# Two attentions of a two-block network: where the softmax scaling runs, how its row statistics are grouped, and how the gates' bias is made

## The chip, the core and the metric

One Trainium2 chip, one core. The metric is the device time of one execution in microseconds, as the median of several runs. The engines of the core are TensorE (PE, with PEld for its weight loads), VectorE (DVE), ScalarE (ACT), GpSimd (POOL) and SyncE (SP), each with its own queue of instructions that it runs in order.

## What is computed

A residual network of depth 2 twice over, on 256 tokens of width 1024, in float32: first a short convolution and an RWKV mixer, each followed by an MLP, then two attentions, each followed by an MLP. The change touches the two attentions alone. Both have 16 heads of 64 and work in two blocks of 128 queries. Cut to what matters:

```python
def dsa_attention(xn, w_in, w_o):            # q, k with rotary position; 4 key heads
    score = einsum(relu(qi . ki), wi)        # an indexer of 8 heads
    _, sel = top_k(where(admissible, score, -inf), 64)
    logits = qg . k[sel] * scale             # masked where a key was not selected
    p = softmax(logits)
    return (p @ v[sel]) @ w_o

def shared_kv(h, g_kv, w_kv, b_f):           # log of the forget gates, summed over the tokens
    cum = cumsum(log_sigmoid(f_logit + b_f))

def fox_attention(xn, w_q, w_o, k, v, cum):
    logits = q . k * scale
    decay = cum[query] - cum[key]
    logits = where(key_pos <= query_pos, logits + decay, -inf)
    p = softmax(logits)
    return (p @ v) @ w_o
```

A term that is the same for all keys of a query, such as `cum[query]`, cancels in the softmax.

## The kernel before

Activations lie transposed, features on the partitions and the 256 tokens along the row. A linear layer reads weights in units of 128x1024. SP loads them in pairs, ACT rounds a unit to the short format (L357, `HL`), DVE takes the remainder (L359), and PE makes each product in three short matmuls (L393 to L395). Units are split three ahead of their use, four split units have room (`HLB`), and three PSUM banks (`mm`) take the results of linear layers.

The code emits the linear layers and the work that hangs on their results interleaved: `drive` emits `per` steps of the linear layer (4 in the first attention, 5 in the second; a step is three matmuls), then one step of each active generator, up to its next `yield`. A planner then orders each engine's queue by this order of emission and by its own estimates of durations, with the weight splits given a head start; the chip runs the queues as they are.

In both attentions the query projection is a linear layer of 8 units, and each unit gives a pair of heads. For a pair, `attend` emits: the scores on PE into PSUM (L828 for the first 128 queries against 128 keys, L829 for the second 128 against all 256); on DVE, for each head and block, the bias added and the row's maximum (L836, which writes `lg`), then the maximum scaled (L839, `nm`); on ACT the exponentials with their sums (L844); on DVE the reciprocal (L847, `rs`) and the scaling of `lg` by it (L849), one instruction for 128x128 and one for 128x256 a head; on PE the transposes (L855); on ACT their copy (L857); on PE the product with the values (L862, L863); on ACT and DVE the split of the result (L865, L866). `lg` has four buffers, enough for two pairs.

In the first attention (`dsa`, called DSA below) the indexer's top-k runs on DVE before the first maximum can be taken; the mask `madd` (L1010) is the bias of all heads. The queries are rotated: DVE makes one product (L934), POOL the other (L933) and their sum `q` (L935), for which the scores wait. In the second (`fox`) the bias is made for each head on DVE (L1126) from the gates of the keys `cb` (broadcast to all partitions by a DMA through DRAM, L1096), those of the queries `cq` (two transposes on PE, L1100, and L1101) and the causal mask `cm`. POOL has no work there.

Of the kernel before, what the change touches and what calls it, by code (L numbers as in the profile page):

```python
# [6 lines left out]
F32 = mybir.dt.float32  # L7
F32R = mybir.dt.float32r
AF = mybir.ActivationFunctionType
OP = mybir.AluOpType  # L10
# [159 lines left out]
def att_consts():  # L170

    d = np.arange(128) % 64
    inv = (1.0 / (10000.0 ** (np.arange(0, 64, 2, dtype=np.float32) / np.float32(64)))).astype(np.float32)
    ang = (np.arange(T, dtype=np.float32)[None] * inv[d // 2][:, None]).astype(np.float32)
    cos, sin = np.cos(ang), np.sin(ang) * np.where(d % 2, 1, -1)[:, None]
    q = np.arange(128)[:, None]
    causal = [np.where(np.arange(w)[None] <= q + o, 0.0, -1e30) for w, o in ((128, 0), (256, 128))]
    return np.concatenate([cos, sin] + causal, axis=1).astype(np.float32)


def stage_units(stage, I):
# [30 lines left out]
def layout(I, stages):  # L212
# [11 lines left out]
    for i in ADAPE:  # L224
# [12 lines left out]
        "cc": col(I["c"].reshape(-1)),  # L237
    }
    a["attc"] = att_consts()
    a["wf"] = I["w_kv_b_2"][:, 2 * D:].reshape(KT, 128, 16).transpose(1, 0, 2).reshape(128, KT * 16)  # L240
    a["wa2"] = np.concatenate([I["rw_w2"][0], I["rw_a2"][0]], axis=0)
# [11 lines left out]
class Prog:  # L253
# [559 lines left out]
        s.at = cx.enter_context(s.tc.tile_pool(name="at", bufs=2))  # L813
        s.at1 = cx.enter_context(s.tc.tile_pool(name="at1", bufs=1))

    def attend(s, i, q, k, v, bias):


        nc = s.nc
        mm, tr = nc.tensor.matmul, nc.tensor.transpose  # L820
        V, A, G = nc.vector, nc.scalar, nc.gpsimd
        E2 = range(2)
        r = [slice(64 * e, 64 * e + 64) for e in E2]
        parts = ((0, 128), (128, 384))
        lg, m, nm, sm, rs, w, ps = ({} for _ in range(7))
        for e in E2:
            ps[e] = s.axbank()
            mm(ps[e][:, 0:128], q[r[e], 0:128], k(e)[:, 0:128], start=True, stop=True)  # L828
            mm(ps[e][:, 128:384], q[r[e], 128:256], k(e), start=True, stop=True)  # L829
        yield  # L830
        for e in E2:
            bb = bias(e)
            lg[e] = s.at.tile([128, 384], F32, name="lg", bufs=4)
            m[e] = s.at.tile([128, 2], F32, name="m", bufs=4)
            for j, (a, b) in enumerate(parts):
                V.tensor_tensor_reduce(lg[e][:, a:b], ps[e][:, a:b], bb[j], scale=1.0, scalar=-3e38, op0=OP.add, op1=OP.max,  # L836
                                       accum_out=m[e][:, j:j + 1])
            nm[e] = s.at.tile([128, 2], F32, name="nm", bufs=4)
            V.tensor_scalar(nm[e], m[e], -0.125, None, op0=OP.mult)  # L839
        yield  # L840
        for e in E2:
            sm[e] = s.at.tile([128, 2], F32, name="sm", bufs=4)
            for j, (a, b) in enumerate(parts):
                A.activation(lg[e][:, a:b], lg[e][:, a:b], AF.Exp, bias=nm[e][:, j:j + 1], scale=0.125,  # L844
                             accum_out=sm[e][:, j:j + 1])
            rs[e] = s.at.tile([128, 2], F32, name="rs", bufs=4)
            V.reciprocal(rs[e], sm[e])  # L847
            for j, (a, b) in enumerate(parts):
                V.tensor_scalar(lg[e][:, a:b], lg[e][:, a:b], rs[e][:, j:j + 1], None, op0=OP.mult)  # L849
            yield  # L850

        for e in E2:
            pt = s.axbank()
            for j in range(3):
                tr(pt[:, 128 * j:128 * j + 128], lg[e][:, 128 * j:128 * j + 128], s.ident)  # L855
            w[e] = s.at.tile([128, 384], F32, name="pt", bufs=4)
            A.activation(w[e], pt[:, :384], AF.Copy)  # L857
        yield
        po = s.axbank()
        for e in E2:  # L860
            kw = dict(tile_position=(0, 64 * e))
            mm(po[r[e], :T], v(e, 0), w[e][:, 0:256], start=True, stop=False, **kw)  # L862
            mm(po[r[e], 128:T], v(e, 1), w[e][:, 256:384], start=False, stop=True, **kw)  # L863
        yield
        A.activation(s.yh[:, i], po[:, :T], AF.Copy)  # L865
        V.tensor_tensor(s.yl[:, i], po[:, :T], s.yh[:, i].bitcast(F32), op=OP.subtract)  # L866
# [21 lines left out]
    def dsa(s, after):  # L888
        nc, tc = s.nc, s.tc
        mm, tr = nc.tensor.matmul, nc.tensor.transpose  # L890
        V, A, G = nc.vector, nc.scalar, nc.gpsimd
        with ExitStack() as cx:
            s.attn_pool(cx)
            at, one = s.at, s.at1
# [3 lines left out]
            ps = s.axbank()  # L898
# [25 lines left out]
            def swapped(raw, n=2):  # L924

                t = s.t("rs")
                for e in range(2):
                    (nc.sync, A, G)[RPQ[e]].dma_start(t[e:64 * n:2], raw[1 - e:64 * n:2])
                return t

            def rope(dst, raw, sw, e):
                u = s.t("ru")
                (V, G)[RPE[e]].tensor_tensor(u, sw, sn, op=OP.mult)  # L933
                V.tensor_tensor(dst, raw, ct, op=OP.mult)  # L934
                (V, G)[RPE[e + 2]].tensor_tensor(dst, dst, u, op=OP.add)  # L935
# [46 lines left out]
            madd = sc[:, 1]  # L982
# [47 lines left out]
            def ev_q(m, ps):  # L1030
                raw = s.t("raw")
                A.activation(raw, ps[:, :T], AF.Copy)
                sw = swapped(raw)
                yield RPW[2]
                q = at.tile([128, T], F32, name="q", bufs=3)
                rope(q, raw, sw, 1)
                yield
                n = m // 2
                s.finish_gen(idx)
                yield from s.attend(m, q, lambda e: kd[64 * e:64 * e + 64, n],  # L1040
                         lambda e, j: vr[:, n // 2, j, 64 * (n % 2):64 * (n % 2) + 64],
                         lambda e: (madd[:, 0:128], madd[:, 128:384]))
            lin(8, ev_q, head=HQ)
        after()
        s.out_proj()
# [15 lines left out]
    def fox(s, after):  # L1061
        nc, tc = s.nc, s.tc
        mm, tr = nc.tensor.matmul, nc.tensor.transpose
        V, A, G = nc.vector, nc.scalar, nc.gpsimd
        with ExitStack() as cx:
            s.attn_pool(cx)
            at, one = s.at, s.at1
            cm = one.tile([128, 384], F32, name="cm")
            G.dma_start(cm, s.d["attc"][:, 2 * T:])
            wf = one.tile([128, KT, 16], F32, name="wf")  # L1070
            G.dma_start(wf.rearrange("p a b -> p (a b)"), s.d["wf"])
# [6 lines left out]
            ps = s.axbank()  # L1078
            for kt in range(KT):
                s.mm3(ps[:16, :T], (wfs[:, 0], wfs[:, 1]), kt, zh[:, kt, :T], zl[:, kt, :T], kt == 0, kt == KT - 1)  # L1080
            f = one.tile([16, 4, T], F32, name="f")
# [12 lines left out]
            nc.sync.dma_start(cd, f[:, 3])  # L1094
            cb = s.big.tile([128, 16, T], F32, name="cb", tag="h1")
            nc.sync.dma_start(cb, bass.AP(tensor=cd.tensor, offset=cd.offset, ap=[[0, 128], [T, 16], [1, T]]))  # L1096
            cq = one.tile([128, 2, 16], F32, name="cq")
            pt = s.axbank()
            for j in range(2):
                tr(pt[:, 16 * j:16 * j + 16], f[:, 3, 128 * j:128 * j + 128], s.ident[:16, :16])  # L1100
            V.tensor_scalar(cq, pt[:, :32].rearrange("p (a b) -> p a b", a=2), -1.0, None, op0=OP.mult)  # L1101
            lin = lambda n, ev, **kw: s.linear(n, lambda k: zh[:, k, :T], lambda k: zl[:, k, :T], ev, per=PERF, **kw)
            kT = one.tile([128, 8, T], F32, name="kT")
            vr = one.tile([128, 8, 2, 128], F32, name="vr")
# [13 lines left out]
            def ev_q(m, ps):  # L1118
                q = at.tile([128, T], F32, name="q", bufs=3)
                V.tensor_tensor(q, ps[:, :T], s.rstd[:, :T], op=OP.mult)  # L1120

                def bias(e):
                    h = 2 * m + e
                    b = at.tile([128, 384], F32, name="fb", bufs=3)
                    for j, (a, w) in enumerate(((0, 128), (128, 256))):
                        V.scalar_tensor_tensor(b[:, a:a + w], cb[:, h, :w], cq[:, j, h:h + 1], cm[:, a:a + w], op0=OP.add,  # L1126
                                               op1=OP.add)
                    return b[:, 0:128], b[:, 128:384]
                yield
                yield from s.attend(m, q, lambda e: kT[64 * e:64 * e + 64, m], lambda e, j: vr[:, m, j, 64 * e:64 * e + 64], bias)  # L1130
            s.linear(8, lambda k: zq[:, 0, k], lambda k: zq[:, 1, k], ev_q, head=HFQ, per=PERF)
# [649 lines left out]
```

## Time and profile before

| what | value |
|---|---|
| median of 3 runs | 1428.42 us (1427.44 to 1430.31) |
| the profiled execution | 1418.36 us |
| its span in the trace | 1416.6 us |
| PE, DVE, ACT, POOL busy | 95%, 70%, 52%, 9% of the span |

The profiled execution is one more execution, 10.06 us below the median of the runs; 1.8 us of its time lie outside the span. The trace tells of that execution alone. DSA's attention proper lies at 846 to 900 us of the span, fox's stage at 1105 to 1207 us, and its attention proper from 1156 us on.

### The profile page before, as it was taken

The numbers are of one execution on the slowest core, as the hardware profiler recorded it, in microseconds if no ns is written. First come the engines' busy times: TensorE is split into PE (matmuls) and PEld (weight loads), VectorE is DVE, ScalarE is ACT, GpSimd is POOL, SyncE is SP. The second block draws the span as 40 slices with busy tenths as digits, with TensorE's granted clock in tenths as the row PEclk, the third lists the DMA queues.
The fourth block names the chain that finished last, engine by engine and source line by source line (L and its number), as shares of the span: only waits on it lengthen the run. The fifth ranks groups of instructions, "written<-read, shape, count | busy, mean of one in ns | idle before, by whom it ended". The sixth has DMA issues, their size and how long they took to land.

```text
span 1416.6 us, 26025 instructions
## 1 busy us (share of the span) xinstructions
PE 1349.4 (95%) x10420; PEld 1290.1 (91%) x10420; DVE 994.1 (70%) x1937; ACT 742.4 (52%) x1424; POOL 132.9 (9%) x157
## 2 busy tenths in 40 slices
PE   6999999997969999999999998999999999999997
PEld 6999999996859998899999986899999987999997
DVE  3699998757875876687566679755557668655554
ACT  3445664842524442267377545674565456673663
POOL 0000000003460212100000254000000000000000
PEclk9999999998989999999999999999999999999999
DMA  8688898556733210266555444355555651455552
GB/s 322 234 329 292 311 324 292 189 199 251 284 133 120 83 53 16 68 220 202 197 185 179 158 143 142 102 183 199 181 179 188 227 181 61 149 208 180 183 198 95
DMA packets 46904, 263.38 MB, mean 186 GB/s; under 512 B 5472, under 2 KB 9776, under 8 KB 20800
## 3 DMA queue, kind: packets, MB, share of 16 engines
q1 hardware_dynamic: 46432, 260.97, 51.9%
q8 instruction: 82, 1.34, 0.4%
q0 software_dynamic: 208, 0.59, 0.1%
q14 instruction: 38, 0.31, 0.1%
q10 hardware_dynamic: 144, 0.16, 0.1%
HBM read 257.69 MB, written 2.11 MB: 183 GB/s over the span
## 4 chain that ended last, share of the span: by engine, by line
PE 76%; DVE 13%; POOL 3%; DMA 3%; issue 2%; ACT 2%; POOLq 0%; DVEq 0%; SPq 0%; ACTq 0%
PE mm L394 19%; PE mm L393 19%; PE mm L395 19%; DVE HL L359 3%; PE mm L391 2%; DVE adu L553 2%; PE mm L430 2%; PE ax L430 1%; DMA raw<-in_w_dram 1%; DMA adu<-in_ada_dram 1%; PE ax L569 1%; PE ax L862 1%; POOL R L1321 1%; PE ax L1372 1%; DMA rs<-raw 1%
## 5 line engine op out<-in xcount | busy, mean ns | idle before, releaser
L359 DVE TENSOR_TENSOR HL<-raw,HL 128x1024 fp32r<-128x1024 f32 x348 | 426.8, 1233 | 226.0 <-ACT HL L357 225.7
L357 ACT ACTIVATE HL<-raw 128x1024 fp32r<-128x1024 f32 x348 | 364.3, 1056 | 281.5 <-PE mm L395 214.9
L395 PE MATMUL mm<-zh,HL 128*128 128x256 f32 (+1 forms) x1328 | 376.5, 284 | 5.5 <-DVE HL L359 5.4
L393 PE MATMUL mm<-zh,HL 128*128 128x256 f32 (+1 forms) x1328 | 377.0, 284 | 2.7 <-ACT cv L663 1.2
L394 PE MATMUL mm<-zl,HL 128*128 128x256 f32 (+1 forms) x1328 | 375.6, 283 | 0.0
L394 PE MATMUL mm<-hlo,HL 128*128 128x256 f32 x1024 | 288.1, 281 | 0.0
L395 PE MATMUL mm<-hh,HL 128*128 128x256 f32 x1024 | 287.8, 281 | 0.0
L393 PE MATMUL mm<-hh,HL 128*128 128x256 f32 x1024 | 285.5, 279 | 0.0
L395 PEld LDWEIGHTS mm<-zh,HL 128*128 128x128 f32 x1328 | 251.9, 190 | 6.9 <-DVE HL L359 6.8
L393 PEld LDWEIGHTS mm<-zh,HL 128*128 128x128 f32 x1328 | 251.8, 190 | 6.1 <-issue 2.4
L394 PEld LDWEIGHTS mm<-zl,HL 128*128 128x128 f32 x1328 | 252.6, 190 | 0.0
L393 PEld LDWEIGHTS mm<-hh,HL 128*128 128x128 f32 x1024 | 193.5, 189 | 0.0
L394 PEld LDWEIGHTS mm<-hlo,HL 128*128 128x128 f32 x1024 | 192.7, 188 | 0.1
L395 PEld LDWEIGHTS mm<-hh,HL 128*128 128x128 f32 x1024 | 192.5, 188 | 0.0
L553 DVE CUSTOM_DVE_ANT_0 adu<-adu,cact,cols 128x1024 f32<-128x1024 f32 x67 | 84.9, 1280 | 0.6 <-DMA adu<-in_ada_dram 0.6
L393 PE MATMUL mm<-yh,HL 128*128 128x256 f32 x256 | 75.5, 297 | 3.1 <-DVE x L718 2.2
L394 PE MATMUL mm<-yl,HL 128*128 128x256 f32 x256 | 74.2, 292 | 0.0
L395 PE MATMUL mm<-yh,HL 128*128 128x256 f32 x256 | 73.8, 289 | 0.0
L523 POOL TENSOR_TENSOR r<-r,mhalf 128x2 f32<-128x2 f32 x6 | 6.3, 1047 | 675.0 <-DVE r L518 542.2
L761 DVE TENSOR_TENSOR hlo<-ma,hh 128x256 fp32r<-128x256 f32 x128 | 53.5, 422 | 5.8 <-ACT hh L758 3.1
L758 ACT ACTIVATE hh<-ma 128x256 fp32r<-128x256 f32 x128 | 52.9, 417 | 3.5
L393 PEld LDWEIGHTS mm<-yh,HL 128*128 128x128 f32 x256 | 50.1, 196 | 4.6 <-issue 3.2
(437 smaller groups left out, 2104.0 us busy)
## 6 DMA issues: line engine op xcount, KB each, us to landing
raw<-in_w_dram SPq DMA_DIRECT2D x177, 1024.0 KB, 4.9
adu<-in_ada_dram SPq DMA_DIRECT2D x72, 512.0 KB, 7.7
rawh<-in_w_dram SPq DMA_DIRECT2D x13, 1024.0 KB, 6.2
raw<-in_ada_dram SPq DMA_DIRECT2D x12, 1024.0 KB, 6.1
cb<-cd SPq DMA_DIRECT2D x1, 2048.0 KB, 10.9
rs<-raw SPq DMA_DIRECT2D x28, 64.0 KB, 1.9
x<-in_x_dram SPq DMA_DIRECT2D x4, 256.0 KB, 4.6
R<-in_wa_dram SPq DMA_DIRECT2D x2, 512.0 KB, 6.8
```

Of the source, the lines that this page charges most:

```text
L357: s.nc.scalar.activation(h, raw, AF.Copy)
L359: s.nc.vector.tensor_tensor(l, raw, h.bitcast(F32), op=OP.subtract)
L391: mm(ps, H[:, kt], rh, start=start, stop=stop)
L393: mm(ps, H[:, kt], rh, start=start, stop=False)
L394: mm(ps, H[:, kt], rl, start=False, stop=False)
L395: mm(ps, L[:, kt], rh, start=False, stop=stop)
L430: s.nc.tensor.matmul(ps[j][:, :N], a, b[:, k], start=kt == i == 0, stop=kt == 7 and i == len(ab) - 1)
L553: s.nc.vector.tensor_tensor_reduce(t, t, s.cact, scale=1.0, scalar=s.c("adab", i), op0=OP.mult, op1=OP.add, accum_out=s.modf[:, i:i + 1])
L569: s.nc.tensor.matmul(ps, w[:, k], s.ccol[:, k:k + 1], start=k == 0, stop=k == KT - 1)
L758: nc.scalar.activation(s.hh[:, m], a, AF.Copy)
L761: nc.vector.tensor_tensor(s.hlo[:, m], a, s.hh[:, m].bitcast(F32), op=OP.subtract)
L862: mm(po[r[e], :T], v(e, 0), w[e][:, 0:256], start=True, stop=False, **kw)
```

## The change

It does four things. The scaling of the exponentials moves from DVE to POOL, for both heads of a pair in fox and for the first head in DSA, where the second stays on DVE (`on_v`). The four maxima, sums and reciprocals of a pair share one tile each, so one instruction scales four maxima and one takes four reciprocals; with that the exponentials of the first head wait for the maxima of both, and the scaling of the first head for the sums of both. In fox the bias of a head is no longer made for each head: two additions over all 16 heads add the causal mask to the first 128 keys' gates (into a new tile `c0`) and to the last 128 (in `cb` itself), and the queries' gates with their two transposes are left out. The causal mask in DRAM is 128 columns wide in place of 384.

```diff
-    causal = [np.where(np.arange(w)[None] <= q + o, 0.0, -1e30) for w, o in ((128, 0), (256, 128))]
-    return np.concatenate([cos, sin] + causal, axis=1).astype(np.float32)
+    causal = np.where(np.arange(128)[None] <= q, 0.0, -1e30)
+    return np.concatenate([cos, sin, causal], axis=1).astype(np.float32)
...
-    def attend(s, i, q, k, v, bias):
+    def attend(s, i, q, k, v, bias, on_v=()):
...
+        m, nm, sm, rs = (s.at.tile([128, 4], F32, name=n, bufs=3) for n in ("m", "nm", "sm", "rs"))
...
             lg[e] = s.at.tile([128, 384], F32, name="lg", bufs=4)
-            m[e] = s.at.tile([128, 2], F32, name="m", bufs=4)
             for j, (a, b) in enumerate(parts):
                 V.tensor_tensor_reduce(lg[e][:, a:b], ps[e][:, a:b], bb[j], scale=1.0, scalar=-3e38, op0=OP.add, op1=OP.max,
-                                       accum_out=m[e][:, j:j + 1])
-            nm[e] = s.at.tile([128, 2], F32, name="nm", bufs=4)
-            V.tensor_scalar(nm[e], m[e], -0.125, None, op0=OP.mult)
+                                       accum_out=m[:, 2 * e + j:2 * e + j + 1])
+        V.tensor_scalar(nm, m, -0.125, None, op0=OP.mult)
         yield
         for e in E2:
-            sm[e] = s.at.tile([128, 2], F32, name="sm", bufs=4)
             for j, (a, b) in enumerate(parts):
-                A.activation(lg[e][:, a:b], lg[e][:, a:b], AF.Exp, bias=nm[e][:, j:j + 1], scale=0.125,
-                             accum_out=sm[e][:, j:j + 1])
-            rs[e] = s.at.tile([128, 2], F32, name="rs", bufs=4)
-            V.reciprocal(rs[e], sm[e])
+                n = slice(2 * e + j, 2 * e + j + 1)
+                A.activation(lg[e][:, a:b], lg[e][:, a:b], AF.Exp, bias=nm[:, n], scale=0.125, accum_out=sm[:, n])
+        V.reciprocal(rs, sm)
+        for e in E2:
             for j, (a, b) in enumerate(parts):
-                V.tensor_scalar(lg[e][:, a:b], lg[e][:, a:b], rs[e][:, j:j + 1], None, op0=OP.mult)
+                (V if e in on_v else G).tensor_scalar(lg[e][:, a:b], lg[e][:, a:b], rs[:, 2 * e + j:2 * e + j + 1], None, op0=OP.mult)
             yield
...
-                         lambda e: (madd[:, 0:128], madd[:, 128:384]))
+                         lambda e: (madd[:, 0:128], madd[:, 128:384]), on_v=(1,))
...
-            cm = one.tile([128, 384], F32, name="cm")
+            cm = one.tile([128, 128], F32, name="cm")
...
-            cq = one.tile([128, 2, 16], F32, name="cq")
-            pt = s.axbank()
-            for j in range(2):
-                tr(pt[:, 16 * j:16 * j + 16], f[:, 3, 128 * j:128 * j + 128], s.ident[:16, :16])
-            V.tensor_scalar(cq, pt[:, :32].rearrange("p (a b) -> p a b", a=2), -1.0, None, op0=OP.mult)
+            c0 = one.tile([128, 16, 128], F32, name="c0")
+            tri = cm[:, None, :].to_broadcast([128, 16, 128])
+            V.tensor_tensor(c0, cb[:, :, :128], tri, op=OP.add)
+            V.tensor_tensor(cb[:, :, 128:], cb[:, :, 128:], tri, op=OP.add)
...
                 def bias(e):
                     h = 2 * m + e
-                    b = at.tile([128, 384], F32, name="fb", bufs=3)
-                    for j, (a, w) in enumerate(((0, 128), (128, 256))):
-                        V.scalar_tensor_tensor(b[:, a:a + w], cb[:, h, :w], cq[:, j, h:h + 1], cm[:, a:a + w], op0=OP.add,
-                                               op1=OP.add)
-                    return b[:, 0:128], b[:, 128:384]
+                    return c0[:, h], cb[:, h]
```

## Rows read from the trace of the kernel before

**Rows 1.** The page's first part: busy time, share of the span and instructions by engine.
```profile
PE 1349.4 (95%) x10420; PEld 1290.1 (91%) x10420; DVE 994.1 (70%) x1937; ACT 742.4 (52%) x1424; POOL 132.9 (9%) x157
```
**Rows 2.** Windows: span; PE, PEld, DVE, ACT, POOL busy (instructions); clock, DMA share, GB/s.
```profile
858.40:867.00 8.60, 5.22 (x45) 4.44 (x46) 7.80 (x31) 5.74 (x21) 4.26 (x4) 1.00 0.45 154
867.00:871.00 4.00, 4.00 (x24) 3.27 (x24) 3.28 (x17) 1.82 (x5) 0.92 (x2) 0.58 0.69 262
871.00:880.00 9.00, 8.17 (x70) 6.34 (x67) 8.26 (x31) 6.44 (x19) 5.87 (x7) 1.00 0.08 27
880.00:900.00 20.00, 19.89 (x139) 14.43 (x138) 14.67 (x74) 14.62 (x53) 1.89 (x3) 1.00 0.16 55
...
1125.00:1156.00 31.00, 31.00 (x172) 26.79 (x171) 16.36 (x21) 13.05 (x15) 0.00 (x0) 1.00 0.64 233
...
1168.00:1176.00 8.00, 7.51 (x61) 6.45 (x61) 7.95 (x33) 4.28 (x10) 0.00 (x0) 1.00 0.16 57
1176.00:1190.00 14.00, 14.00 (x118) 11.22 (x116) 13.62 (x61) 12.05 (x40) 0.00 (x0) 1.00 0.11 44
1190.00:1207.00 17.00, 16.93 (x114) 12.34 (x113) 11.17 (x51) 8.91 (x30) 0.00 (x0) 1.00 0.19 63
```
**Rows 3.** Waits of PE, 846 to 900 us: total, times, longest.
```profile
PE ax L828 <- POOL q L935: 3.4, 2, 2.0
```
**Rows 4.** Timeline of DSA: start, duration, instruction, idle before and its releaser.
```profile
864.50 0.42 DVE L934 TENSOR_TENSOR q<-raw,tabs 128x256 f32<-128x256 f32 x1
...
864.91 1.22 DVE L359 TENSOR_TENSOR HL<-raw,HL 128x1024 fp32r<-128x1024 f32 x1
865.06 1.64 POOL L935 TENSOR_TENSOR q<-q,ru 128x256 f32<-128x256 f32 x1 [4.34 <-DVE nm L839]
...
866.76 0.50 PE L828 MATMUL ax<-kd,q 64*128 64x128 f32 x4 [2.03 <-POOL q L935]
```
**Rows 5.** Groups of DVE by form, 855 to 897 us: busy us, mean ns.
```profile
L849 DVE TENSOR_SCALAR lg<-lg,rs 128x256 f32<-128x256 f32 x16 | 6.0, 376 | 0.0
L849 DVE TENSOR_SCALAR lg<-lg,rs 128x128 f32<-128x128 f32 x16 | 5.0, 310 | 0.1
...
L847 DVE RECIPROCAL rs<-sm 128x2 f32<-128x2 f32 x16 | 2.5, 159 | 1.6 <-ACT lg L844 1.4
```
**Rows 6.** Lines L934, L839 and L935: ns min/median/max, first and last start.
```profile
L934 DVE TENSOR_TENSOR q<-raw,tabs x8: 399/422/878, 849.9 to 881.0; 128x256 f32<-128x256 f32 x8
L839 DVE TENSOR_SCALAR nm<-m x32: 148/161/687, 860.1 to 1197.3; 128x2 f32<-128x2 f32 x32
L935 POOL TENSOR_TENSOR q<-q,ru x8: 782/1231/1847, 850.4 to 881.9; 128x256 f32<-128x256 f32 x8
```
**Rows 7.** Scalings on POOL elsewhere (RWKV), L1256 with constants, L1288 with two columns.
```profile
L1256 POOL TENSOR_SCALAR txt<-txt x8: 397/404/1158, 353.6 to 395.3; 128x256 f32<-128x256 f32 x8
L1288 POOL TENSOR_SCALAR R<-txt,cols,small x8: 596/621/1911, 354.1 to 396.7; 128x256 f32<-128x256 f32 x8
```
**Rows 8.** Groups of DVE by form, 1156 to 1210 us (fox).
```profile
L1126 DVE SCALAR_TENSOR_TENSOR fb<-cb,cq,cm 128x256 f32<-128x256 f32 x13 | 6.2, 480 | 0.0
...
L1126 DVE SCALAR_TENSOR_TENSOR fb<-cb,cq,cm 128x128 f32<-128x128 f32 x13 | 4.5, 343 | 0.0
```
**Rows 9.** Waits of PE, 1100 to 1210 us (fox).
```profile
PE ax L855 <- DVE m L836: 0.5, 1, 0.5
```
**Rows 10.** Timeline of PE around L1100.
```profile
1116.01 0.28 PE L394 MATMUL mm<-zl,HL 128*128 128x256 f32 x1
1116.13 0.28 PE L395 MATMUL mm<-zh,HL 128*128 128x256 f32 x1
...
1116.93 0.39 PE L393 MATMUL mm<-zh,HL 128*128 128x256 f32 x1
```
**Rows 11.** The gates' broadcast L1096, and who waited for it: us, times.
```profile
  DVE fb L1126: 0.7, 1
...
DMA to landing us min/median/max: 10.9/10.9/10.9
```

More of the change, by code (lines that the diff above doesn't have):

```diff
@@ L824, in attend @@
         parts = ((0, 128), (128, 384))
-        lg, m, nm, sm, rs, w, ps = ({} for _ in range(7))
+        lg, w, ps = ({} for _ in range(3))
+        m, nm, sm, rs = (s.at.tile([128, 4], F32, name=n, bufs=3) for n in ("m", "nm", "sm", "rs"))
         for e in E2:
```

## The prediction

> **What bounds the kernel now.** I read the page's first part first: PE is busy 95% of the span, DVE 70%, POOL 9% [rows 1]. A time can only come off where PE waits. So I next cut the two attentions into windows and look at PE's busy time against the length of each, with DVE's beside it [rows 2]. The reader is to see two different stages. In fox DVE is as full as it can be (7.95 of 8.00 us, 13.62 of 14.00), and yet PE loses only 0.49, 0.00 and 0.07 us in the three windows: the planner kept enough other matmuls in front of PE. Fox is bound by PE, with DVE just behind it. In DSA, once the indexer is done, PE loses 8.60 - 5.22 = 3.38 us, then runs 4.00 us at a granted clock of 0.58, so partly at the lower of its two levels, then loses 0.83 and 0.11 us. The low clock is worth at most (1 - 0.58) x 4.00 = 1.7 us. All that a faster softmax could give back in DSA is thus 3.38 + 1.7 + 0.83 + 0.11 = 6.0 us. Last I ask who ends these waits. It is one pair of engines: PE's scores wait 3.4 us in two waits for the rotated queries from POOL [rows 3]. The longer of them, 2.03 us, has POOL itself idle for 4.34 us because DVE reaches the product L934 only at 864.50, after a queue of maxima, scalings and a weight split [rows 4]. There DVE is what ends last, at 7.80 of 8.60 us busy [rows 2].
>
> **Fox, the bias.** DVE is rid of 16 x (480 + 343) ns = 13.2 us [rows 8] (13 of the 16 heads show in that window). It gets two additions over 2048 columns. None of that size stands in the trace; the split L359 over 1024 columns takes 1.22 us [rows 4], so 1.2 to 2.45 us each, and I take 2.3, since the columns are twice as many. They wait for the gates' broadcast, 10.9 us from issue, for which the bias waited 0.7 us before [rows 11]. Queued behind them on DVE are a PSUM evacuation and the splits of the value units. DVE is busy 16.36 of 31.00 us there while PE is full [rows 2], so 2 x 2.3 + 0.7 = 5.3 us fit, and I price them at nothing; without that cover they would cost PE up to 5.3 us, less whatever split units lie ready. The smaller load of the mask sits in POOL's queue behind nothing that is used soon: nothing.
>
> **Fox, the two transposes of the queries' gates.** They go from PE. PE's last matmul before them starts at 1116.13 and its next at 1116.93 [rows 10]: 0.80 us, of which an ordinary matmul's step stays, 0.12 from 1116.01 to 1116.13 in the same rows. Bounds 0 (something else is late there) and 0.7; I take 0.6, since the queue behind holds only ready matmuls.
>
> **Fox, the scaling and the shared statistics.** DVE loses, by DSA's prices, 16 x (376 + 310) ns = 11.0 us of scaling and 8 x (161 + 159) ns = 2.6 us of small instructions [rows 5, 6]. With the bias that is 27 us, which makes DVE loose. PE's one wait for DVE there, 0.5 us at L855 [rows 9], goes. POOL gets four scalings a pair. Its price by the nearest rows: 128x256 takes 404 ns with constants and 621 ns with two columns [rows 7]; one column lies between, I take 0.5, and 0.3 for 128x128. A pair is 1.6 us on POOL against 1.4 on DVE, and at worst four times the 1.91 us maximum, 7.6 us. PE needs about 51 us for 8 pairs, 6.4 us a pair, so POOL doesn't bind at its ordinary price. The chain of a pair gets longer by the second head's maxima and exponentials, but it no longer stands in DVE's queue. What is late next is PE itself. Fox in all: -0.6 - 0.5 = -1.1 us, bounds -1.3 and +2 (two or three pairs' transposes late by the 0.7 to 1.3 us that a held POOL scaling costs over a free one).
>
> **DSA, what leaves DVE.** A pair's first head takes 376 + 310 ns with it and the merged statistics 161 + 159 ns: 1.0 us a pair [rows 5, 6]. In the window that holds the long wait, one pair's whole softmax stands ahead of L934, so the product comes 1.0 us sooner and the wait of 2.03 us falls to 1.0. The other wait of the two stands ahead of the first softmax and stays. In the next windows DVE is 8.26 of 9.00 us full [rows 2] and loses some 1.5 us; the hole of 0.83 us there I take as closed, -0.8 (bounds 0 and -0.83). The clock: through the window up to 867 it was 1.00, although PE had already waited 3.4 - 2.0 = 1.4 us once, and it fell only behind the second, longer hole [rows 2, 3]. A hole of 1.0 us is nearer to the first, so I take the whole 1.7 us as given back (bounds 0 and -1.7).
>
> **DSA, what is added.** POOL gets two scalings a pair, 0.8 us free, and the first head waits for both heads' maxima and sums. The transposes behind them come later; for the first two pairs, where PE has least else to do, I take +0.25 us each, +0.5 (bounds 0, where linear matmuls cover it, and 2 x 1.2 us, a held scaling). Queued behind the scalings on POOL are the next pairs' rotations, for which PE's scores wait; that is the second rival. DSA in all: -1.0 - 0.8 - 1.7 + 0.5 = -3.0 us.
>
> **A rule that speaks against it.** DVE and POOL hold each other up in this trace. The sum L935 takes 782 ns at best and 1847 at worst, and 1.64 us where it ran beside the split L359 [rows 4, 6]; DVE's product L934 goes from 399 to 878 ns and the small L839 from 148 to 687 [rows 6]. The Trainium skill says why, in SBUF — State Buffer, section "Who interferes with whom": the two share a pair of SBUF ports, a DVE instruction with two SBUF inputs or in a two-port mode contends with POOL, and whoever starts first holds the pair for the whole instruction. The trace agrees with its blocking: 1.64 us beside a split against 0.78 alone. By that rule the moved work would partly come back as blocking; the first rival works this out from the rows.
>
> **The rivals.**
> *The lock eats it.* Each of the two POOL scalings a pair holds a DVE instruction once, for 0.48 us (L934) or 0.54 us (L839): 2 x 0.5 = 1.0 us a pair against 1.0 us saved. DVE is as late as before, DSA gives nothing, fox -1.1: 1427.3 us. For it: the collisions are in the very stretch. Against it: a scaling is short, and the split, at 1.22 us the longest, is more often the holder than the held.
> *POOL becomes the bound in DSA (slower).* POOL is busy 5.87 of 9.00 us at 871 to 880 [rows 2]; 1.5 pairs of scalings add 1.2 us free and 1.5 x (1.16 + 1.91) = 4.6 us at the maxima [rows 7], which is full. Its queue is in order: a scaling that waits for four exponentials and a reciprocal, planned ahead of a later pair's rotation, holds that rotation, and PE's scores with it. If 6 pairs lose what a held L935 costs over a free one, 1.64 - 0.78 = 0.86 us, that is +5.2 us, with fox +4.1: 1432.5 us. It decides from the point where the reciprocal of a pair comes later than the product L934 of the pair whose rotation stands behind it. Against it: only half the scaling goes to POOL here.
> *DSA loses all its holes.* -6.0 - 1.1 = -7.1: 1421.3 us. For it: the whole 6.0 us lie behind a full DVE. Against it: the first wait of 1.4 us has nothing to do with the softmax.
> *DVE never mattered.* That is the first rival's time, since fox hides it already.
>
> **How the numbers follow.** -1.1 - 3.0 = -4.1 us. The profiled execution would go from 1418.36 to 1414.3 us; the runs' median stands 10.06 us above it, and I carry that over: 1428.42 - 4.1 = 1424.3 us. A measurement of this kernel can tell about 0.2%, 2.9 us, from no change, so faster means below 1425.6. Chances: the forecast (1422.5 to 1426) 0.42, of which 0.34 below 1425.6; the lock 0.26; POOL bound 0.20, of which 0.02 within 0.2%; all holes closed 0.12. Faster 0.46, same 0.36, slower 0.18. The range leaves out the upper half of the slower rival and the lower end of the best case: 1420.8 to 1431.5.
>
> **What would show it.** In the profile after: DVE's busy time in fox's attention down by over 20 us, with PE's wait at L855 and the hole at 1116 gone; in DSA the wait of the scores for `q` down to one of 1.4 and one of about 1 us, no window at a clock below 1.00 behind it, and POOL scalings near 0.5 and 0.3 us. I am wrong if scores wait longer for POOL, if transposes L855 wait for `lg` from POOL, or if DVE's L359 and L934 take much longer than 1.22 and 0.42 us.

## The result, and the profile after

The changed kernel took 1433.74 us in the median of 6 executions (1432.47 to 1436.86), the kernel before 1428.65 us on the same chip (6 executions). By the medians that is 5.09 us or 0.36% more. The ratio on record, which is not the quotient of the medians, is 1.0057, with a 95% interval of 1.0032 to 1.0082: slower by either, beyond the top of the stated range (1431.5), and close to the time of the slower rival (1432.5). One execution of the run `fast_all` below took 2940.8 us, about twice any other, and is left out of that run's ratio.

The page's first part answers to [rows 1]: DVE's busy time fell by 19 us, POOL's rose by 41.

```profile
span 1435.1 us, 26003 instructions
## 1 busy us (share of the span) xinstructions
PE 1359.3 (95%) x10418; PEld 1295.8 (90%) x10418; DVE 975.5 (68%) x1826; ACT 743.4 (52%) x1424; POOL 174.2 (12%) x205
```

The two profiled spans, 1416.6 and 1435.1 us, are not to be subtracted as a whole. The first instruction of the DSA stage on DVE (L902) starts at 803.8 us before and at 815.1 us after, and nothing ahead of it was changed. In a second profile of the unchanged kernel (the run `again`, below) it starts at 807.8. Single executions of one kernel scatter by over 1% (the kernel before ran from 1412.52 to 1431.44 us in one comparison), and the granted clock over the span was 0.983, 0.974 and, in that second profile, 0.980; so times are compared here as medians of many executions, and stages of single profiles by marks of their own.

Two instructions serve as marks: the last one that makes DSA's mask (L1010) and the first one on fox's gates (L1083). From the one to the other I call the DSA stretch, from the second to the end of the span the fox stretch. The kernel before, then the changed one, each by the first start of the two lines:

```profile
L1010 DVE TENSOR_SCALAR sc<-sc x1: 354/354/354, 858.0 to 858.0; 128x384 f32<-128x384 f32 x1
L1083 DVE TENSOR_TENSOR f<-ax,rstd x1: 413/413/413, 1110.4 to 1110.4; 16x256 f32<-16x256 f32 x1
```
```profile
L1010 DVE TENSOR_SCALAR sc<-sc x1: 352/352/352, 868.7 to 868.7; 128x384 f32<-128x384 f32 x1
L1083 DVE TENSOR_TENSOR f<-ax,rstd x1: 411/411/411, 1128.7 to 1128.7; 16x256 f32<-16x256 f32 x1
```

The DSA stretch went from 1110.4 - 858.0 = 252.4 us to 1128.7 - 868.7 = 260.0 us. The fox stretch went from 1416.6 - 1110.4 = 306.2 to 1435.1 - 1128.7 = 306.4 us. The whole loss, 7.6 us in this execution, lies in DSA; fox came out even.

PE's waits, first of 846 to 920 us, then of 1120 to 1230 us (total, times, longest), answer to [rows 3, 9]. The lines of the scores, L828 and L829 before, are L831 and L832 now; the transposes are L855 in both:

```profile
PE ax L855 <- POOL lg L849: 8.2, 10, 2.4
PE ax L831 <- POOL q L935: 1.3, 1, 1.3
PE mm L395 <- DVE HL L359: 0.6, 1, 0.6
```
```profile
PE ax L855 <- POOL lg L849: 3.2, 6, 0.9
PE ax L527 <- POOL r L523: 0.5, 1, 0.5
```

The scores wait for POOL's rotation once in place of twice, as forecast. But the transposes L855 now wait for the scaled exponentials from POOL, 8.2 us in DSA and 3.2 us in fox, where before they waited for POOL not at all. The windows, in the columns of [rows 2], show the same place: POOL full at 876 to 882 us, PE losing 1.42, 2.97 and 3.57 us in windows of DSA and 2.60 and 1.13 us in fox, and the clock clearly below 1.00 twice.

```profile
876.00:882.00 6.00, 4.58 (x24) 3.16 (x26) 3.67 (x16) 2.78 (x7) 5.84 (x8) 0.72 0.58 197
882.00:890.00 8.00, 7.97 (x68) 6.13 (x64) 5.74 (x21) 5.76 (x20) 4.39 (x6) 0.99 0.49 165
890.00:900.00 10.00, 7.03 (x42) 4.63 (x41) 5.88 (x26) 5.84 (x20) 5.26 (x7) 0.83 0.00 0
900.00:918.00 18.00, 14.43 (x102) 9.99 (x100) 7.02 (x33) 9.94 (x36) 6.09 (x8) 1.00 0.00 1
...
1190.00:1210.00 20.00, 17.40 (x140) 13.46 (x140) 12.01 (x54) 14.92 (x49) 13.72 (x15) 1.00 0.27 85
1210.00:1226.00 16.00, 14.87 (x119) 12.11 (x119) 4.16 (x20) 7.97 (x27) 8.40 (x12) 1.00 0.07 28
```

The longest wait, in the timeline (start, duration, instruction, idle before):

```profile
891.46 0.18 DVE L846 RECIPROCAL rs<-sm 128x4 f32<-128x4 f32 x1
...
892.27 0.72 POOL L933 TENSOR_TENSOR ru<-rs,tabs 128x256 f32<-128x256 f32 x1 [1.09 <-DMA rs<-raw]
...
892.94 1.21 DVE L359 TENSOR_TENSOR HL<-raw,HL 128x1024 fp32r<-128x1024 f32 x1
892.97 2.54 POOL L849 TENSOR_SCALAR lg<-lg,rs 128x128 f32<-128x128 f32 x2
...
894.67 0.33 PE L855 MATMUL ax<-ident,lg 128*128 128x128 f32 x1 [2.40 <-POOL lg L849]
```

The reciprocal is done at 891.64. On POOL a rotation stands ahead of the scaling and waits for its DMA; then the scaling runs beside a weight split, and its two instructions take 2.54 us. On DVE the second head's scaling, behind the same reciprocal, had run from 891.87 to 892.41. So this longest wait holds three things: the rotation in front, the split beside, and the price of the scalings themselves.

Line L849 as a whole (ns min/median/max) and POOL's share of it by form (busy us, mean ns):

```profile
L849 POOL TENSOR_SCALAR lg<-lg,rs x48: 598/918/1962, 875.9 to 1218.7; 128x128 f32<-128x128 f32 x24, 128x256 f32<-128x256 f32 x24
L849 DVE TENSOR_SCALAR lg<-lg,rs x16: 280/379/530, 876.1 to 914.1; 128x128 f32<-128x128 f32 x8, 128x256 f32<-128x256 f32 x8
```
```profile
L849 POOL TENSOR_SCALAR lg<-lg,rs 128x256 f32<-128x256 f32 x24 | 25.4, 1059 | 0.0
L849 POOL TENSOR_SCALAR lg<-lg,rs 128x128 f32<-128x128 f32 x24 | 17.2, 718 | 83.1 <-DVE rs L846 82.5 <-PE ax L855 0.6
```

A scaling of 128x256 on POOL cost 1.06 us in the mean, one of 128x128 0.72 us; I had put 0.5 and 0.3. POOL as a whole was not short of time: for five of DSA's eight pairs it stood idle ahead of the scaling. The same line, up to 920 us (total, times):

```profile
its engine sat idle before it (us, times) until:
  DVE rs L846: 16.8, 5
```

There the scaling is late by its own length in a pair's chain (scores, maxima, exponentials, reciprocal, scaling, transposes), not by a queue on POOL.

### The profile page after: what moved, and what is told of

The parts are those of the page before. It is cut to its first block, busy times and chain, and to the rows that moved or that the text cites. A ratio compares the mean times of both kernels' runs of the same rounds, so it can differ in the third digit from the quotient of the medians.

```text
span 1435.1 us, 26003 instructions
## 1 busy us (share of the span) xinstructions
PE 1359.3 (95%) x10418; PEld 1295.8 (90%) x10418; DVE 975.5 (68%) x1826; ACT 743.4 (52%) x1424; POOL 174.2 (12%) x205
## 4 chain that ended last, share of the span: by engine, by line
PE 61%; issue 17%; DVE 12%; POOL 5%; DMA 3%; ACT 2%; POOLq 0%; DVEq 0%; SPq 0%; ACTq 0%
PE mm L394 14%; PE mm L393 14%; PE mm L395 14%; DVE HL L359 3%; PE mm L391 3%; POOL lg L849 2%; DVE adu L553 2%; PE ax L430 2%; PE mm L430 1%; DMA raw<-in_w_dram 1%; PE ax L569 1%; DMA adu<-in_ada_dram 1%; POOL R L1316 1%; PE ax L1367 1%; DMA rs<-raw 1%
## 5 line engine op out<-in xcount | busy, mean ns | idle before, releaser
L359 DVE TENSOR_TENSOR HL<-raw,HL 128x1024 fp32r<-128x1024 f32 x348 | 425.2, 1228 | 224.2 <-ACT HL L357 224.0
```

What stands on the lines that cost most here:

```text
L359: s.nc.vector.tensor_tensor(l, raw, h.bitcast(F32), op=OP.subtract)
```

## The experiments

My theory after the result: the price of one scaling on POOL, twice what I had put, sets when the transposes can run. The rivals: the shared statistics make a pair's chain too long; any work on POOL is late, by its queue and the shared ports; and the difference is only the clock's chance. But for the single executions and the first comparison (6 against 6), the medians are of 12 executions against 23 or 35 of the kernel before on the same chip; the stretches are those of the one profiled execution (in `stats_only` the two marks are L1009 and L1082).

| run | median | before | ratio, interval | DSA stretch | fox stretch |
|---|---|---|---|---|---|
| before | | | | 252.4 | 306.2 |
| again | 1422.23 (one) | 1425.71 | | 252.3 | 306.8 |
| the change | 1433.74 | 1428.65 | 1.0057, 1.0032 to 1.0082 | 260.0 | 306.4 |
| probe | 1428.98 (one) | 1425.71 | | | |
| all_v | 1422.15 | 1425.71 | 0.9977, 0.9961 to 0.9994 | 249.0 | 302.5 |
| move_only | 1430.53 | 1425.71 | 1.0044, 1.0018 to 1.0069 | 255.0 | 307.1 |
| fast_all | 1422.54 | 1425.99 | 0.9966, 0.9941 to 0.9991 | 252.4 | 303.4 |
| dsa_v | 1426.24 | 1425.99 | 1.0010, 0.9988 to 1.0031 | 249.4 | 307.1 |
| fox_v | 1427.67 | 1425.99 | 1.0007, 0.9979 to 1.0035 | 258.8 | 302.2 |
| bias_only | 1423.38 | 1425.99 | 0.9970, 0.9946 to 0.9994 | 252.2 | 302.9 |
| stats_only | 1424.22 | 1426.83 | 0.9981, 0.9946 to 1.0016 | 252.9 | 304.5 |
| move_fast | 1425.76 | 1426.83 | 0.9993, 0.9968 to 1.0019 | 252.6 | 305.4 |

**The unchanged kernel once more.** No edit.

> The kernel before once more, unchanged, for a second profile. Theory A (the two single profiles differ before the attentions by chance of the clock, so they can't be subtracted as a whole): this profile again lies up to 11 us apart from the first one in the RWKV stage, which the change doesn't touch, and its attentions keep their places: in DSA PE waits about 3.4 us for the rotated queries and not at all for lg. Theory B (the change itself slows RWKV): this profile has the RWKV stage of the first profile of before to within 1 us.

Theory A of this run: the stage ahead of DSA moved by 4.0 us (L902 at 807.8 for 803.8), and the stretches stayed within 0.1 and 0.6 us. The waits of the scores are the same, 3.4 us in two. One thing differs. The window that answers to the low-clock one of [rows 2], taken at the same distance from L1010, and the one behind it:

```profile
870.30:874.30 4.00, 4.00 (x35) 3.24 (x36) 3.22 (x17) 2.11 (x7) 0.92 (x2) 1.00 0.75 262
874.30:883.30 9.00, 7.31 (x58) 5.72 (x59) 8.85 (x31) 6.27 (x19) 6.07 (x7) 1.00 0.09 31
```

Behind the same 2.0 us hole the clock stayed at 1.00 here, PE did 35 matmuls in place of 24, and then lost 1.69 us in the next window in place of 0.83. The stretch took as long. So the low clock was neither caused by that hole alone nor worth 1.7 us: PE ran ahead and then stood.

**The price of a scaling by itself.** Nine forms on an unused tile, five times each, added to the kernel before. Their code stands in fox, but they ran at 910 to 957 us, right behind DSA's attention:

```diff
+            for _ in range(5):
+                G.tensor_scalar(sx, sx, sk[:, 0:1], None, op0=OP.mult)
+                G.tensor_scalar(sy, sx, sk[:, 0:1], None, op0=OP.mult)
+                G.tensor_scalar(sx, sx, sk[:, 0:1], 0.0, op0=OP.mult, op1=OP.add)
+                G.tensor_scalar(sx, sx, sk[:, 0:1], sk[:, 1:2], op0=OP.mult, op1=OP.mult)
+                G.tensor_scalar(sx, sx, 1.0, None, op0=OP.mult)
+                G.tensor_scalar(sx, sx, 1.0, 0.0, op0=OP.mult, op1=OP.add)
+                G.tensor_tensor(sx, sx, sk[:, 0:1].to_broadcast([128, 256]), op=OP.mult)
+                G.tensor_scalar(sx[:, :128], sx[:, :128], sk[:, 0:1], None, op0=OP.mult)
+                G.tensor_scalar(sx[:, :128], sx[:, :128], sk[:, 0:1], 0.0, op0=OP.mult, op1=OP.add)
```

> The kernel before, with nine forms of scaling on GpSimd added on a scratch tile in fox, five times each, whose results nobody uses. Theory A (a scaling by one column with no second operation has a slow form of its own on POOL): 128x256 takes 0.92 us free and 128x128 0.60 us, as in the changed kernel, while the same with a second operation (times the column, plus 0.0) takes 0.60 us or less at 128x256, as L1288 with two columns did (0.62). Theory B (operands in place, or this stage, make it slow): all forms with a column take 0.9 us.

The lines of that run in the order of the diff (ns min/median/max; by "free" I mean the executions with little or no DVE work beside them, which give the least times; the longest lie beside weight splits):

```profile
L1109 POOL TENSOR_SCALAR sx<-sx,sk x5: 927/1082/2871, 910.2 to 946.9; 128x256 f32<-128x256 f32 x5
...
L1110 POOL TENSOR_SCALAR sy<-sx,sk x5: 925/926/1987, 911.2 to 949.8; 128x256 f32<-128x256 f32 x5
...
L1111 POOL TENSOR_SCALAR sx<-sx,sk x5: 482/492/882, 912.2 to 950.8; 128x256 f32<-128x256 f32 x5
...
L1112 POOL TENSOR_SCALAR sx<-sx,sk x5: 552/556/1633, 912.8 to 951.4; 128x256 f32<-128x256 f32 x5
...
L1113 POOL TENSOR_SCALAR sx<-sx x5: 851/853/1693, 913.5 to 952.1; 128x256 f32<-128x256 f32 x5
...
L1114 POOL TENSOR_SCALAR sx<-sx x5: 408/807/1211, 914.4 to 953.9; 128x256 f32<-128x256 f32 x5
L1115 POOL TENSOR_TENSOR sx<-sx,sk x5: 615/661/1456, 915.3 to 954.7; 128x256 f32<-128x256 f32 x5
...
L1116 POOL TENSOR_SCALAR sx<-sx,sk x5: 605/902/1703, 916.1 to 955.5; 128x128 f32<-128x128 f32 x5
...
L1117 POOL TENSOR_SCALAR sx<-sx,sk x5: 375/377/1571, 917.1 to 956.3; 128x128 f32<-128x128 f32 x5
```

Theory A: on POOL a scaling with one operation takes 0.93 us at 128x256 and 0.61 us at 128x128; the same with a second operation that does nothing takes 0.48 and 0.38 us. It is not the column (a constant alone takes 0.85) and not the place (into another tile, 0.93). The starts tell the same as the durations: the first round goes 910.2, 911.2, 912.2, 912.8, so the two slow forms take 1.0 us each and the one behind them 0.6. Both rows on which I had based the price, [rows 7], have a second operation.

**All scaling back on DVE.**

```diff
-                (V if e in on_v else G).tensor_scalar(lg[e][:, a:b], ...
+                V.tensor_scalar(lg[e][:, a:b], ...
```

> The changed kernel with all scaling back on DVE; the shared statistics and the new bias stay. Theory A (the price of the scaling on POOL puts the transposes behind it): PE's waits at L855, 8.2 us in DSA and 3.2 us in fox, go, and the time falls below the kernel before, to 1424 to 1428 us. Theory B (the shared statistics make the chain of a pair too long): the time stays at 1432 us or more, and L855 waits for the scaling on DVE instead.

1422.15 against 1425.71 us: faster, with its interval below 1, and below the 1424 to 1428 us expected. The waits at L855 are 1.3 us in DSA, for DVE, and none in fox:

```profile
PE ax L855 <- DVE lg L849: 1.3, 2, 1.1
```

Against the change the two stretches are 11.0 and 3.9 us shorter. Theory A; the shared statistics are not what made the change slow.

**The scaling alone moved**, in the kernel before, with the old statistics and bias.

```diff
-                V.tensor_scalar(lg[e][:, a:b], lg[e][:, a:b], rs[e][:, j:j + 1], None, op0=OP.mult)
+                (V if e in on_v else G).tensor_scalar(lg[e][:, a:b], lg[e][:, a:b], rs[e][:, j:j + 1], None, op0=OP.mult)
```

> The kernel before with only the scaling moved to POOL as in the change; statistics for each head and the old bias. Theory A (price of the scaling on POOL): slower than before by 4 to 8 us, with PE's waits at L855 for lg from POOL of 8 us or more. Theory B (shared statistics): within 2 us of before.

Slower, by 0.44% (0.18% to 0.69%): the move alone is a loss. The waits at L855, in DSA and in fox, are 2.9 + 1.6 = 4.5 us, not 8 or more:

```profile
PE ax L855 <- POOL lg L849: 2.9, 4, 1.4
```
```profile
PE ax L855 <- POOL lg L849: 1.6, 3, 1.1
```

So part of the change's 11.4 us seems to need the move and the shared statistics together (one profile of each).

**A second operation in the scalings on POOL**, the only edit to the changed kernel. Every engine holds the same instructions in the same order as in the changed kernel, so that nothing differs but the time that these 48 take.

```diff
-  rs[:, 2 * e + j:2 * e + j + 1], None, op0=OP.mult)
+  rs[:, 2 * e + j:2 * e + j + 1], None if e in on_v else 0.0, op0=OP.mult, **({} if e in on_v else dict(op1=OP.add)))
```

> The changed kernel with a second operation, plus 0.0, in the scalings on POOL; nothing else. Theory A (the price of one scaling, 0.92 and 0.60 us where 0.48 and 0.38 were to be had, makes PE wait): PE's waits at L855 for lg fall from 11.4 us in the two attentions to under 5 us, and the time falls by 4 us or more below the changed kernel, to that of before or under it. Theory B (any scaling on POOL is late, because its queue also holds the rotations and waits for all four exponentials): the waits at L855 stay above 8 us and the time within 2 us of the changed kernel's, 4 us or more above before.

1422.54 us for 1433.74 (beside them the kernel before took 1425.99 and 1428.65), and faster than before (0.9966, 0.9941 to 0.9991). L849 on POOL, PE's waits in the two attentions, and the two marks, in a span of 1421.3 us:

```profile
L849 POOL TENSOR_SCALAR lg<-lg,rs x48: 372/478/1515, 872.7 to 1205.2; 128x128 f32<-128x128 f32 x24, 128x256 f32<-128x256 f32 x24
```
```profile
PE ax L831 <- POOL q L935: 1.3, 1, 1.3
PE ax L855 <- POOL lg L849: 1.3, 4, 0.6
```
```profile
L1010 DVE TENSOR_SCALAR sc<-sc x1: 350/350/350, 865.5 to 865.5; 128x384 f32<-128x384 f32 x1
L1083 DVE TENSOR_TENSOR f<-ax,rstd x1: 411/411/411, 1117.9 to 1117.9; 16x256 f32<-16x256 f32 x1
```

The waits for POOL at L855 fell from 11.4 to 1.3 us and the stretches by 7.6 and 3.0 us. Theory A, by the cleanest of these runs: same queues, same ports, same chain of statistics, another price.

**The same form for the move alone.** `move_only` with that second operation.

> The kernel before with the scaling moved to POOL in the form with a second operation, plus 0.0; statistics for each head, old bias. Theory A (price): the 4.5 us of waits at L855 of the same move in the slow form fall under 1.5 us, and the time is within 2 us of before or below it. Theory B (moving to POOL costs by itself, by its order and the shared ports): 4 us or more above before.

Within the measurement of before (0.9993, 0.9968 to 1.0019), with 0.6 us of waits at L855 for POOL. Moving the scaling alone, in the cheaper form, neither costs nor gives anything that 12 executions can tell.

**DSA alone on DVE, and fox alone on DVE.**

```diff
-  on_v=(1,))                   # dsa_v, DSA
+  on_v=(0, 1))
-  bias)                        # fox_v, fox
+  bias, on_v=(0, 1))
```

> The changed kernel with DSA's scaling all on DVE; fox's stays on POOL. Theory A: the loss of the change sits in DSA, where PE has least other work and POOL also rotates queries; without it DSA's attention ends about 5 us sooner than before, fox keeps its 3.2 us of waits at L855, and the time is 2 to 5 us below before. Theory C (fox's four scalings a pair are the loss): still 3 us or more above before.

> The changed kernel with fox's scaling all on DVE; DSA's first head stays on POOL. Theory A (the loss sits in DSA): PE's 8.2 us of waits at L855 in DSA stay, fox gains about 3 us on before, and the time is 1 to 3 us above before. Theory C (the loss sits in fox): at least 2 us below before.

The stretches part cleanly: DSA 249.4 and 258.8 us, fox 307.1 and 302.2 us. The scaling on POOL costs about 9 us in DSA and 5 us in fox against DVE. PE's waits at L855 for POOL are 2.3 us in `dsa_v`, all in fox, and 7.1 us in `fox_v`, all in DSA. My expectation that the loss sits in DSA alone fell: the executions of both are within 0.1% of before, where `dsa_v` was to be 2 to 5 us below it. Fox loses with POOL what the bias gives it. These runs also show how far the stretches repeat, since the scaling runs on the same engine in pairs of them: DSA on POOL 260.0 and 258.8 us (the change, `fox_v`), DSA on DVE 249.0 and 249.4 (`all_v`, `dsa_v`), fox on POOL 306.4 and 307.1 (the change, `dsa_v`), fox on DVE 302.5 and 302.2 (`all_v`, `fox_v`).

**The bias alone.** The two additions, the narrow mask and no `cq`, in the kernel before (the diff's part in `att_consts` and `fox`).

> The kernel before with the new bias alone: two additions in place of 32 instructions on DVE, and no transposes of the queries' gates. By the prediction's step this gives 0.6 us for the transposes and 0.5 us for the wait at L855, about 1 us. If DVE's load in fox held PE back more than its waits showed, 3 us or more. In no theory is it slower than before by over 1 us.

Faster by 0.30% (0.06% to 0.54%), with the fox stretch 3.3 us shorter, not 1. In no row of waits do those 3.3 us stand: before had 0.5 us at L855 and the hole of 0.7 us around L1100. Added up over the fox stretch, PE's idle time went only from 4.1 to 3.8 us.

**The shared statistics alone.** The diff's part in `attend`, with all scaling on DVE.

> The kernel before with only the shared statistics: four maxima scaled and four reciprocals taken at once, all scaling on DVE, the old bias. Theory A (the price of the POOL scaling is the whole loss): within 2 us of before, 2.6 us of DVE's work saved against a chain that is longer by the second head's maxima and sums. Theory B (the shared statistics cost time by themselves): 3 us or more above before, with PE's waits at L855 grown from 0.5 us.

Not told apart from before (0.9946 to 1.0016), as theory A has it, though the median is 2.6 us below and not within 2. Fox is 1.7 us shorter. DSA, at 252.9 us, holds the same code as in `all_v` at 249.0; in this execution the clock there fell:

```profile
866.00:890.00 24.00, 21.38 (x145) 16.86 (x144) 20.60 (x71) 14.96 (x48) 10.54 (x11) 0.86 0.47 154
```

(1 - 0.86) x 24 us is 3.4 us, about the difference. So where the clock differs, two profiles of the same DSA code can lie 3 to 4 us apart, and a difference of that size between two stretches shows nothing by itself.

## Why the prediction was wrong, step by step

**What bounds the kernel.** That reading held in the main. Fox is PE's and DSA has holes behind a full DVE: `all_v`, which takes only small instructions and the bias off DVE, gained 3.4 and 3.7 us in the two stretches (`dsa_v` 3.0 us in DSA; `stats_only`, at a lower clock, nothing there). But its premise, that a time can only come off where PE waits, did not hold in fox, as told below.

**The price of a scaling on POOL: the step that failed.** I put 0.5 and 0.3 us between two rows of POOL scalings [rows 7] and called one column "between" constants and two columns. The free price was 0.93 and 0.61 us, outside both ends. The rows were near in shape and operands, but both carry a second operation, and the moved instruction has none. A pair in fox cost 3.1 us on POOL free, in place of 1.6, and a first head in DSA 1.5 us in place of 0.8. `fast_all` shows that this alone made the loss: at 0.48 and 0.38 us, near the price that I had put, and with nothing else moved, the kernel is faster than before. Its median lies 3.5 us below before, where the forecast was 4.1. That nearness is luck in the terms: in its profile DSA gives nothing (252.4 us) and fox 2.8 us, where I had put 3.0 and 1.1.

**DSA, what is added.** I allowed 0.5 us, at most 2.4 us, for later transposes, for the first two pairs only. The transposes waited 8.2 us in ten places, to the last pairs. The bound took the price from the wrong rows, and it took the later pairs to be covered; with the true price they were not. In the cheaper form (`fast_all`) these waits were 1.3 us in four places, within the bound.

**DSA, what leaves DVE.** The second of the two waits for the rotated queries went, as the step said (3.4 us in two to 1.3 in one). It went in `all_v` and `stats_only` too, where the scaling stays on DVE (1.3 us in one), and in `move_fast`, with the old statistics (1.4 us in one): either part of the change was enough.

**The clock.** I counted 1.7 us as given back. `again` has the same hole with the clock at 1.00 and the same stretch of 252.3 us, so nothing was there to give. After the change the clock was lower in two windows (0.72 and 0.83), worth (1 - 0.72) x 6 + (1 - 0.83) x 10 = 3.4 us at most; in `fox_v`, with the same code in DSA, it was lower in the same places (10 to 30 us behind the mask it was 0.83 and 0.85 in the change, 0.83 and 0.87 there), and in `fast_all` not. Two profiles are few; how much of it belongs to the change stays open.

**Fox.** The two additions took what I had worked out from L359, and hid behind PE as said; the first one's line, with its wait for the broadcast:

```profile
L1099 DVE TENSOR_TENSOR c<-cb,cm x1: 2294/2294/2294, 1147.1 to 1147.1; 128x2048 f32<-128x2048 f32 x1
...
  DMA cb<-cd: 0.5, 1
```

The transposes gave what was put: from the second mark to fox's first scores it was 1160.7 - 1110.4 = 50.3 us before and 1178.2 - 1128.7 = 49.5 after, 0.8 us for 0.6. The sign that DVE's busy time in fox's attention falls by over 20 us did not come. From the second mark to the end of the span, before and after:

```profile
1110.40:1416.60 306.20, 295.88 (x2362) 281.36 (x2360) 191.89 (x386) 171.14 (x319) 0.70 (x1) 0.99 0.47 166
```
```profile
1128.70:1435.10 306.40, 293.20 (x2359) 279.94 (x2358) 178.21 (x307) 170.88 (x319) 28.78 (x33) 0.99 0.47 165
```

It fell by 13.7 us. I had added up durations, and those of all DVE instructions there do add up to 21.1 us less; but neighbours overlap in the trace.

And -1.1 us for fox was a third of what the bias alone gave (3.3 us). I had counted PE's waits only. Most of the 3.3 us lies in PE's busy time, 295.88 us before and 292.99 us in `bias_only`. Counted in the traces of `before` and `bias_only`, PE goes from one kind of matmul to another (by tile: linear, scores, transposes, values) 116 and 100 times in the fox stretch, and the step from the last matmul before such a change to the next takes 0.20 us in the mean, idle time left out, against 0.12 us between two linear matmuls. That gives an estimate of 16 x 0.08 = 1.3 us; with 0.4 us less of idle time, the cause of about 1.6 of the 3.3 us stays open.

**The rule on the shared ports.** What the first rival builds on is seen: beside a split a POOL scaling of 128x256 took up to 1.96 us, against 0.92 free. But the Trainium skill's rule, in SBUF — State Buffer, section "Who interferes with whom", is not what decided: `fast_all` keeps the same neighbours in the same order, still has scalings of up to 1.5 us beside splits, and is faster than before. Nor did the first rival's time come.

**The slower rival.** The time, 1433.74 us, came 1.2 us from its 1432.5, but by another way, so that is luck. POOL was full in one window of DSA (5.84 of 6.00 us at 876 to 882), and idle ahead of most later scalings (16.8 us in five waits for the reciprocal). I had PE's scores wait for a rotation behind a scaling, and PE's transposes waited for the scaling itself, sometimes behind a rotation (the timeline at 892). I gave it 0.20 for want of a price from the right row.

Three versions beat both kernels: `fast_all` (0.9966), `bias_only` (0.9970) and `all_v` (0.9977) are faster than before. These runs don't tell which of the three is best; `all_v` and `bias_only` need nothing of POOL, and `bias_only` not even the shared statistics.

## What to carry to other kernels

Before an instruction is moved to another engine, price it by a row of that engine with the same number of operations, not only the same shape and operands; where the trace has none, run the form by itself, on an unused tile, before the sum is made. And ask first whether the work must move at all: here leaving it where it was, with the new bias, with or without the shared statistics, could not be told from moving it in the cheaper form. Where single profiles scatter by more than the effect, measure each stage between marks of its own, and test a price by a kernel whose queues stay the same.

## What the runs showed of the hardware

On POOL a `tensor_scalar` with one operation is slower than with two: 0.93 against 0.48 us at 128x256 and 0.61 against 0.38 us at 128x128 by a column, 0.85 against 0.41 us by a constant (the last is the one of five that ran with nothing on DVE beside it). With the cheaper form the changed kernel's median fell from 1433.74 to 1422.54 us. A multiplication with a column that is spread by its access pattern, `tensor_tensor`, took 0.62 us at 128x256, also less than the scaling with one operation. On DVE the same scaling took 0.38 us at 128x256 in the mean [rows 5].
